# Attention's diagonal blocks multiplied with the 128 columns that count instead of 256

## The chip, the cores and the metric

The kernel runs on one core of a Trainium2 chip. The metric is the time of one execution in device microseconds (us). The time before is the median of three runs.

## What is computed

A decoder trunk of two layers over one sequence of 512 tokens with 2048 features, in float32. Layer 0 is differential attention: 8 heads, each with two components of queries and keys (128 wide) and one set of values (256 wide). Layer 1 is forgetting attention with 16 heads that are 128 wide; its keys, values and forget gates are projected once from the output of layer 0. Both attentions are causal. Cut to what matters here:

```
# layer 0, for block i of 128 queries, head h, component c
sc = q[i] @ k.T + alibi_bias             # (128 x 512), only keys s <= t count
p_c = softmax(where(causal, sc, -1e30))
o[i] = (p_0 - lam * p_1) @ v             # then rms_norm, silu gate, output projection
# layer 1, for block i of 128 queries, head h
sc = q[i] @ k.T + F[t] - F[s]
o[i] = softmax(where(causal, sc, -1e30)) @ v
```

Every layer ends with a residual sum and a LayerNorm; the inputs of the projections are scaled and shifted by vectors that come from a conditioning vector c.

## The kernel before

**Precision.** Each float32 matrix that is multiplied is split into a high and a low part of type float32r (F32R in the code). `products` (L171) then makes three matmuls that add into the same PSUM bank: high by high (L173), high by low (L174) and low by high (L175). Nearly all of the work of TensorE has one of these three lines. Transposes (L720, L767, L1163 and others) the sums of the modulation at the start (L503, L506) and one small product (L237) are the only matmuls that take tiles of plain F32.

**Projections.** `group` multiplies the 2048 x 512 input by 512 columns of weights at a time. It goes through sixteen k-tiles of 128 rows; each burst is two k-tiles for one of four PSUM banks, which is six matmuls of 512 moving columns. The weights come by `WeightStream`: a DMA on SP's queue, a cast on ScalarE (L93) and a subtraction on VectorE (L94).

**Attention, laid between the bursts.** After each burst `tick` runs one entry of the list `pieces`, and for the background products of the modulation one step of a generator. The pieces of a head are its scores, transposes and value products, in an order written out by hand (`attention_a` for layer 0, `attention_pair` for layer 1). So TensorE's order is fixed: six matmuls of a projection, then one piece, and so on.

**Scores.** `score(i)` multiplies query block i by the keys of blocks 0 to i, so w = (i + 1) * 128 columns count. The moving columns are n (layer 0, L692) or m (layer 1), which is w but at least 256. For i = 0 the matmul thus has 256 columns, and what follows on VectorE and ScalarE reads the first 128 of them.

**Values.** Layer 0 keeps the values as moving operand, 256 columns wide, in every block. Layer 1 has the transposed probabilities as moving operand (tiles pTh and pTl, filled by `turn`), and for key block j only queries from j * 128 on count. `values` starts its columns at t0 = min(j * 128, 256) (L1177), so the last block, j = 3, is multiplied with columns 256 to 511, of which the first 128 are blanks: L1090 and L1091 write zeros there once, before layer 1. A comment at L1089 says that this gives the rows 256 columns.

Of the kernel before, what the change touches and what calls it, by code (L numbers as in the profile page):

```python
# [13 lines left out]
ALU = mybir.AluOpType  # L14

P = 128
D = 2048
KT = D // P
T = 512
# [8 lines left out]
# Order of the start, see there: c sums of modulation, m their columns, t a k-tile of h, l its lower part,  # L28
# s a split of weights, g products of a k-tile, digits so many steps of the modulation's sums.
# [4 lines left out]
class Job:  # L34
    """A projection: runs of columns of a 2048-row weight matrix."""
# [14 lines left out]
class WeightStream:  # L50
    """Loads weights two k-tiles at a time and splits them into two float32r parts, ahead of their
    products."""
# [26 lines left out]
    def step(self, extra=None):  # L79
        """Splits the next two k-tiles; extra gives tiles for them outside the stream's own."""  # L80
        job, s = self.order[self.done]
        self.load(self.done + 1)
        st = self.stage[self.done]
        w = job.width
        if extra:
            hi, lo = ([extra() for _ in range(2)] for _ in range(2))
            for k in range(2):
                self.nc.scalar.copy(hi[k][:, :w], st[:, k, :w])
                self.nc.vector.tensor_tensor(lo[k][:, :w], st[:, k, :w], hi[k][:, :w].bitcast(F32), op=ALU.subtract)
        else:  # L90
            hi = self.pool.tile([P, 2, 512], F32R, name="whi", tag="whi", bufs=3)
            lo = self.pool.tile([P, 2, 512], F32R, name="wlo", tag="wlo", bufs=3)
            self.nc.scalar.copy(hi[:, :, :w], st[:, :, :w])  # L93
            self.nc.vector.tensor_tensor(lo[:, :, :w], st[:, :, :w], hi[:, :, :w].bitcast(F32), op=ALU.subtract)  # L94
            hi, lo = ([t[:, k, :] for k in range(2)] for t in (hi, lo))
        self.subs[(id(job), s)] = (hi, lo)
        self.done += 1
# [12 lines left out]
def tile_yoco(  # L110
# [60 lines left out]
    def products(dst, lhs, rhs, start, stop):  # L171
        """dst += lhs^T rhs with lhs and rhs as (hi, lo) parts."""
        PE.matmul(dst, lhs[0], rhs[0], start=start, stop=False)  # L173
        PE.matmul(dst, lhs[0], rhs[1], start=False, stop=False)  # L174
        PE.matmul(dst, lhs[1], rhs[0], start=False, stop=stop)  # L175

    # ---------------------------------------------------------------- constants
# [11 lines left out]
    # rows of parameters, turned into columns by the tensor engine  # L189
# [28 lines left out]
    rows = {}  # L218
# [22 lines left out]
    def rsqrt(y, v, n, pool):  # L241
        """y = v ** -0.5 by Newton steps from an estimate on the exponent."""
        t = pool.tile([P, n], I32, name="rs_t", tag=f"rs_t{n}", bufs=2)
        a = pool.tile([P, n], F32, name="rs_a", tag=f"rs_a{n}", bufs=2)
        h = pool.tile([P, n], F32, name="rs_h", tag=f"rs_h{n}", bufs=2)
        V.tensor_scalar(t, v.bitcast(I32), 1, None, op0=ALU.logical_shift_right)
        V.tensor_scalar(y.bitcast(I32), t, -1.0, float(0x5F3759DF), op0=ALU.mult, op1=ALU.add)
        V.tensor_scalar(h, v, -0.5, None, op0=ALU.mult)
        for _ in range(3):
            if n == 1:  # L250
                V.scalar_tensor_tensor(a, y, h, y, op0=ALU.mult, op1=ALU.mult)
            else:
                V.tensor_tensor(a, y, y, op=ALU.mult)
                V.tensor_tensor(a, a, h, op=ALU.mult)
            V.scalar_tensor_tensor(y, a, 1.5, y, op0=ALU.add, op1=ALU.mult)

    # ---------------------------------------------------------------- weight order
# [3 lines left out]
    # the first two heads: all but the keys of the second component, which follow for both at once  # L261
    first = {h: (Job(a_w_in, [(256 * h, 256), (2048 + 256 * h, 128)]), vg[h]) for h in range(2)}
    kk = Job(a_w_in, [(2048 + 128, 128), (2048 + 384, 128)])
    # k-tiles whose modulation is found together, and the order in which the two heads take k-tiles
# [6 lines left out]
    # the last columns for half of the tokens first, whose LayerNorm is then done ahead of the end  # L271
# [34 lines left out]
    def group(job, natural, evac, banks=range(4), bg=0, before_sub=None, after_sub=None, hold=0, after_held=None):  # L306
        """One projection; natural: tokens on the partitions, else features. The last hold weights
        stay until each bank has had them, one bank after the other."""
# [41 lines left out]
    # modulation vectors as columns [feature, k-tile]  # L350
# [4 lines left out]
    def mod_stream(segs, new_stage, new_acc, nk):  # L355
        """Vector-engine products of silu(c) with columns of a modulation matrix, 512 columns a
        segment; yields after each k-tile."""
# [38 lines left out]
    def mod_row(pool, ones_r, dst, bias, one):  # L396
        """Sums over the partitions, as ones^T acc with acc in two parts; in two steps."""
        def steps(acc):
            hi = pool.tile([P, 512], F32R, name="mhi", tag="mhi", bufs=1)
            lo = pool.tile([P, 512], F32R, name="mlo", tag="mlo", bufs=1)  # L400
            split(hi, lo, acc)
            row = pool.tile([1, 512], F32, name="mrow", tag="mrow", bufs=1)
            nc.sync.dma_start(row, bias.rearrange("(o n) -> o n", o=1))
            yield True
            pt = tr_bank()
            PE.matmul(pt, ones_r, hi, start=True, stop=False)
            PE.matmul(pt, ones_r, lo, start=False, stop=True)
            V.scalar_tensor_tensor(row, pt[0:1, :], one, row, op0=ALU.add, op1=ALU.add)
            nc.sync.dma_start(dst, row)
        return steps  # L410

    # ---------------------------------------------------------------- start: modulation and first projections
    # Shift and scale of sets of k-tiles: sums over silu(c) on the vector engine, for the first sets
    # half of them on the tensor engine. Each k-tile is multiplied for both heads; a head's partial
    # sums wait in SBUF while the other one's are in PSUM.
    part = {}
    with tc.tile_pool(name="start", bufs=2, reuse_waits="tile") as sp, tc.manual_schedule(engines={ET.DVE}):
# [12 lines left out]
        # one entry a tile: set, first k, number of k  # L430
# [53 lines left out]
        def dv(n):  # L484
            """n more products of modulation, none of them past the set after those summed."""
            while n and ahead[0] is not None and ahead[0] <= state["set"]:
                ahead[0] = next(steps, None)
                n -= 1
# [135 lines left out]
    # ---------------------------------------------------------------- layer 0: differential attention  # L624
# [53 lines left out]
    def attention_a(h, lead=3, late=()):  # L678
# [3 lines left out]
        def score(i, comp):  # L682
            def fn():
# [8 lines left out]
                n = max(w, 256)  # L692
# [3 lines left out]
                products(sc[:, :n], (q[0][:, ts], q[1][:, ts]), (k[0][:, :n], k[1][:, :n]), True, True)  # L696
# [110 lines left out]
    # head 1 waits until head 0 is done, and with it the values and gates of head 2  # L807
# [29 lines left out]
    # ---------------------------------------------------------------- output projections and LayerNorm  # L837
# [12 lines left out]
    def out_projection(jobs, layer, zp, opened, residual, norm, after_held=None):  # L850
        """z = residual + gate * y with the statistics of its rows; norm(b) follows a block's last
        columns. zp is filled by opened() once the pieces of the last head have been traced."""
# [43 lines left out]
    # h = x1 * scale + shift on n^T: x1 = n * g + b  # L896
# [19 lines left out]
    def build_half(s, half):  # L916
        """k-tiles 2s and 2s+1 of h for the keys and values, tokens of one half."""
# [17 lines left out]
        # the transposed tokens take the place of the others  # L935
# [3 lines left out]
    # the first values: the tokens of the second half are behind those of the first, which are ready earlier  # L939
# [25 lines left out]
    # ---------------------------------------------------------------- shared keys, values and forget gates  # L965
# [18 lines left out]
    # for each k-tile 64 columns: the two parts of the weights in columns 0-15 and 32-47. The products  # L984
    # take 128 columns, of which those 64 count.
# [26 lines left out]
    def forget_sums():  # L1012
        """-cumsum(min(z, 0) - log1p(exp(-|z|)))"""
# [6 lines left out]
        # log1p(e) = log(w) + (e - (w - 1)) / w  # L1020
# [63 lines left out]
    # ---------------------------------------------------------------- layer 1: forgetting attention  # L1084
# [4 lines left out]
    # the last block of keys is multiplied from query 256 on, so that its rows have 256 columns  # L1089
    V.tensor_scalar(pTh[:, 3, 256:384], mask[:, 0:P], 0.0, None, op0=ALU.mult)  # L1090
    V.tensor_scalar(pTl[:, 3, 256:384], mask[:, 0:P], 0.0, None, op0=ALU.mult)  # L1091
# [39 lines left out]
    def attention_b(hd):  # L1131
        st = {}

        def score(i):
            def fn():
                w = (i + 1) * P
                m = max(w, 256)
# [3 lines left out]
                products(sc[:, :m], (q[0][:, ts], q[1][:, ts]), (k[0][:, :m], k[1][:, :m]), True, True)  # L1141
# [28 lines left out]
        def values(j0, j1):  # L1170
            def fn():
# [4 lines left out]
                for j in range(j0, j1):  # L1176
                    t0 = min(j * P, 256)  # L1177
# [39 lines left out]
    # ---------------------------------------------------------------- layer 1: output projection and LayerNorm  # L1217
# [81 lines left out]
```

## Time and profile before

| | |
|---|---|
| median of three runs | 2016.39 us (2015.3 to 2018.02) |
| span of the profiled execution | 2017.1 us |
| TensorE, matmul instructions | 9115, busy 98% of the span |
| VectorE busy | 66% |
| ScalarE busy | 36% |
| DMA, mean over the span | 175 GB/s |

The times list no time of the profiled execution beside its span; the span is 0.7 us over the median of the three runs and inside their range. In the profile PE is TensorE's matmuls and PEld its weight loads, DVE is VectorE, ACT is ScalarE, SP the engine that issues most DMAs. A group of instructions is named by its tiles as out<-in; of a matmul the moving operand stands first, and 128*128 128x256 means 128 rows and columns of weights and 256 moving columns. The duration of a matmul in the profile overlaps that of the next, so the rate of a stream of matmuls is read from the distance between their starts in the timeline, not from the durations. The layers lie at these times: layer 0's attention from 228 to 860 us, keys and values from about 1030 to 1400 us, layer 1's attention from 1442 to 1857 us.

### The profile page before, as it was taken

The page shows a single profiled execution, that of the slowest core. Times are in us where ns is not written, and L with a number is a line of the kernel's source. Part 1 is how long each engine was busy: PE and PEld are TensorE (multiplying, and loading weights), DVE is VectorE, ACT ScalarE, POOL GpSimd, SP SyncE. Part 2 cuts the span into 40 slices and gives each one's busy share as a digit, 9 for nine tenths or more (in the row PEclk, how much of TensorE's full clock was granted, in tenths as well). Part 3 has the DMA queues.
Part 4 walks back from the last instruction along what each step waited for, and adds up shares of the span by engine and source line. Part 5 has one row for each costly group of instructions (what it writes and reads, how often), then busy time and mean ns, then how long its engine had stood idle before and what let it go on. Part 6 is the DMA issues. An engine that isn't in the chain of part 4 may idle for free.

```text
span 2017.1 us, 25055 instructions
## 1 busy us (share of the span) xinstructions
PE 1967.3 (98%) x9115; PEld 1627.0 (81%) x9115; DVE 1335.3 (66%) x2435; ACT 722.2 (36%) x1230; POOL 2.2 (0%) x10
## 2 busy tenths in 40 slices
PE   5999999999999999999999999999999999999997
PEld 4888878888878888888878877888888888888885
DVE  6887878777667677853575666645455555576678
ACT  2422444423333334431263222224333333453232
POOL 0000000000000000000000000000000000000000
PEclk8999999999999999999999999999999999999999
DMA  9994755564556565452344878733233323232754
GB/s 343 343 316 143 243 172 162 163 224 156 190 167 209 166 221 184 156 165 94 115 138 141 260 255 261 261 124 127 92 102 96 103 91 103 95 118 90 259 193 175
DMA packets 263095, 353.79 MB, mean 175 GB/s; under 512 B 18022, under 2 KB 162556, under 8 KB 262204
## 3 DMA queue, kind: packets, MB, share of 16 engines
q1 hardware_dynamic: 262896, 352.18, 53.3%
q8 instruction: 71, 1.16, 0.2%
q14 instruction: 52, 0.43, 0.1%
q10 hardware_dynamic: 76, 0.02, 0.0%
HBM read 339.47 MB, written 12.66 MB: 175 GB/s over the span
## 4 chain that ended last, share of the span: by engine, by line
PE 81%; DMA 8%; DVE 8%; issue 1%; SPq 1%; ACT 1%; DVEq 0%; ACTq 0%
PE acc L173 23%; PE acc L175 23%; PE acc L174 23%; DMA ms<-in_w_mod_dram 5%; DVE macc L386 2%; DVE wlo L94 2%; PE sc L174 2%; PE sc L175 2%; PE sc L173 2%; DMA sms<-in_w_mod_dram 1%; PE o L175 1%; PE o L174 1%; PE o L173 1%; PE tr L1163 1%; DMA ms<-in_kv_w_mod_dram 1%
## 5 line engine op out<-in xcount | busy, mean ns | idle before, releaser
L93 ACT CAST whi<-wst 128x1024 fp32r<-128x1024 f32 (+2 forms) x339 | 349.6, 1032 | 685.4 <-PE acc L175 315.6
L94 DVE TENSOR_TENSOR wlo<-wst,whi 128x1024 fp32r<-128x1024 f32 (+2 forms) x339 | 404.6, 1196 | 279.9 <-ACT whi L93 265.7
L173 PE MATMUL acc<-whi,hh 128*128 128x512 f32 x1252 | 494.6, 398 | 4.4 <-ACT vt L977 2.9
L174 PE MATMUL acc<-wlo,hh 128*128 128x512 f32 x1252 | 490.6, 392 | 0.1
L175 PE MATMUL acc<-whi,hl 128*128 128x512 f32 x1252 | 489.5, 391 | 0.0
L173 PE MATMUL acc<-hh,whi 128*128 128x512 f32 x1184 | 469.0, 396 | 3.6 <-ACT vt L977 2.9
L174 PE MATMUL acc<-hl,whi 128*128 128x512 f32 x1184 | 462.3, 390 | 0.0
L175 PE MATMUL acc<-hh,wlo 128*128 128x512 f32 x1184 | 462.3, 390 | 0.0
L386 DVE SCALAR_TENSOR_TENSOR macc<-ms,cact,macc 128x512 f32<-128x512 f32 x360 | 270.0, 750 | 116.2 <-DMA ms<-in_w_mod_dram 83.7
L173 PEld LDWEIGHTS acc<-whi,hh 128*128 128x128 f32 x1252 | 236.3, 189 | 51.5 <-ACT vt L977 4.2
L175 PEld LDWEIGHTS acc<-whi,hl 128*128 128x128 f32 x1252 | 235.8, 188 | 51.1 <-DVE hl L934 0.3
L174 PEld LDWEIGHTS acc<-wlo,hh 128*128 128x128 f32 x1252 | 236.2, 189 | 44.3 <-DVE wlo L94 0.5
L173 PEld LDWEIGHTS acc<-hh,whi 128*128 128x128 f32 x1184 | 222.6, 188 | 48.4 <-ACT vt L977 4.1
L175 PEld LDWEIGHTS acc<-hh,wlo 128*128 128x128 f32 x1184 | 222.5, 188 | 48.0
L174 PEld LDWEIGHTS acc<-hl,whi 128*128 128x128 f32 x1184 | 222.8, 188 | 41.1
L476 DVE SCALAR_TENSOR_TENSOR sacc<-sms,cact,sacc 128x512 f32<-128x512 f32 (+1 forms) x127 | 89.5, 705 | 5.9 <-DMA sms<-in_w_mod_dram 2.2
L1152 ACT ACTIVATE eb<-eb,mnb 128x128 f32<-128x128 f32 (+1 forms) x64 | 36.1, 564 | 96.7 <-DVE mnb L1149 95.6
L703 ACT ACTIVATE e<-e,mn 128x128 f32<-128x128 f32 (+3 forms) x64 | 36.1, 563 | 88.7 <-DVE mn L699 88.1
L1149 DVE CUSTOM_DVE_ANT_0 eb<-sc,biasb 128x128 f32<-128x128 f32 (+1 forms) x64 | 31.4, 490 | 52.8 <-PE sc L175 52.8
L1167 DVE TENSOR_TENSOR pTl<-tr,pTh 128x128 fp32r<-128x128 f32 (+1 forms) x64 | 31.2, 487 | 26.5 <-ACT pTh L1166 26.1
L1166 ACT CAST pTh<-tr 128x128 fp32r<-128x128 f32 (+1 forms) x64 | 27.1, 424 | 43.6 <-PE tr L1163 42.9
L769 ACT ACTIVATE ogT<-tr,subg 128x128 f32<-128x128 f32 x64 | 20.0, 364 | 56.0 <-PE tr L767 56.0
(251 smaller groups left out, 1740.0 us busy)
## 6 DMA issues: line engine op xcount, KB each, us to landing
wst<-in_a_w_in_dram SPq DMA_DIRECT2D x240, 256.0 KB
ms<-in_w_mod_dram SPq DMA_DIRECT2D x64, 512.0 KB
ms<-in_kv_w_mod_dram SPq DMA_DIRECT2D x64, 512.0 KB
wst<-in_kv_w_dram SPq DMA_DIRECT2D x64, 512.0 KB
ms<-in_w_mod_dram SPq DMA_DIRECT2D x128, 256.0 KB
wst<-in_b_w_in_dram SPq DMA_DIRECT2D x128, 256.0 KB
sms<-in_w_mod_dram SPq DMA_DIRECT2D x56, 512.0 KB
wst<-in_b_w_out_dram SPq DMA_DIRECT2D x48, 512.0 KB
```

Source lines behind the costliest of these rows:

```text
L93: self.nc.scalar.copy(hi[:, :, :w], st[:, :, :w])
L94: self.nc.vector.tensor_tensor(lo[:, :, :w], st[:, :, :w], hi[:, :, :w].bitcast(F32), op=ALU.subtract)
L173: PE.matmul(dst, lhs[0], rhs[0], start=start, stop=False)
L174: PE.matmul(dst, lhs[0], rhs[1], start=False, stop=False)
L175: PE.matmul(dst, lhs[1], rhs[0], start=False, stop=stop)
L386: V.scalar_tensor_tensor(acc, w, cact[:, kt : kt + 1], acc, op0=ALU.mult, op1=ALU.add)
L476: V.scalar_tensor_tensor(acc, w, sc, acc, op0=ALU.mult, op1=ALU.add)
L703: S.activation(e[:, :w], e[:, :w], AF.Exp, bias=mn, scale=-1.0, accum_out=rs)
L1149: V.tensor_tensor_reduce(out=e[:, :w], in0=sc[:, :w], in1=bias[:, :w], scale=-1.0, scalar=3.0e38, op0=ALU.add, op1=ALU.min, accum_out=mn)
L1152: S.activation(e[:, :w], e[:, :w], AF.Exp, bias=mn, scale=-1.0, accum_out=rs)
L1166: S.copy(pTh[:, 0 : i + 1, ts], src)
L1167: V.tensor_tensor(pTl[:, 0 : i + 1, ts], src, pTh[:, 0 : i + 1, ts].bitcast(F32), op=ALU.subtract)
```

## The change

Three places take the columns that count. `score` in both layers multiplies w columns, so block i = 0 has 128; `values` in layer 1 starts at j * 128, so block j = 3 has 128. The two instructions that wrote zeros into pTh and pTl are gone. The change also blanks comments and docstrings, which moves line numbers by a few.

```diff
@@ attention_a, score
                 w = (i + 1) * P
-                n = max(w, 256)
...
-                products(sc[:, :n], (q[0][:, ts], q[1][:, ts]), (k[0][:, :n], k[1][:, :n]), True, True)
+                products(sc[:, :w], (q[0][:, ts], q[1][:, ts]), (k[0][:, :w], k[1][:, :w]), True, True)
@@ layer 1: forgetting attention
-    # the last block of keys is multiplied from query 256 on, so that its rows have 256 columns
-    V.tensor_scalar(pTh[:, 3, 256:384], mask[:, 0:P], 0.0, None, op0=ALU.mult)
-    V.tensor_scalar(pTl[:, 3, 256:384], mask[:, 0:P], 0.0, None, op0=ALU.mult)
@@ attention_b, score
                 w = (i + 1) * P
-                m = max(w, 256)
...
-                products(sc[:, :m], (q[0][:, ts], q[1][:, ts]), (k[0][:, :m], k[1][:, :m]), True, True)
+                products(sc[:, :w], (q[0][:, ts], q[1][:, ts]), (k[0][:, :w], k[1][:, :w]), True, True)
@@ attention_b, values
-                    t0 = min(j * P, 256)
+                    t0 = j * P
                     products(st["o"][:, t0:], (vh[:, j, es], vl[:, j, es]), (pTh[:, j, t0:], pTl[:, j, t0:]), j == 0, j == 3)
```

## The prediction, made before the result was known

> **What bounds the kernel now.** I read the page of the profile first.
>
> ```profile
> span 2017.1 us, 25055 instructions
> PE 1967.3 (98%) x9115; PEld 1627.0 (81%) x9115; DVE 1335.3 (66%) x2435; ACT 722.2 (36%) x1230; POOL 2.2 (0%) x10
> ...
> PEclk8999999999999999999999999999999999999999
> ...
> PE 81%; DMA 8%; DVE 8%; issue 1%; SPq 1%; ACT 1%; DVEq 0%; ACTq 0%
> ```
>
> TensorE is busy 98% of the span at the full granted clock after the first slice, and its matmuls are 81% of the chain that ended last. That is an average, so I cut out the stretches that the change touches with the windows view: layer 0's attention, the stretch ahead of layer 1 (where the two fills of zeros are), and layer 1's attention. The columns are the window, its length, then busy time and number of instructions of each engine, the granted clock, the DMA share and rate.
>
> ```profile
> 228.00:860.00 632.00, 626.35 (x2968) 520.16 (x2967) 458.51 (x979) 247.18 (x504) 0.00 (x0) 1.00 0.57 182
> 1072.00:1442.00 370.00, 364.21 (x1599) 298.84 (x1598) 213.45 (x267) 104.75 (x128) 0.00 (x0) 1.00 0.61 197
> 1442.00:1857.00 415.00, 414.24 (x1998) 344.75 (x1997) 252.32 (x529) 170.08 (x317) 0.00 (x0) 1.00 0.31 99
> ```
>
> PE is idle 5.65 us of 632 in layer 0 and 0.76 us of 415 in layer 1, while VectorE works 459 and 252 us there. So in both stretches time added to or taken from the row of matmuls reaches the end nearly one for one. The small rest is absorbed where PE waits for something else. In layer 0 the waits view of PE puts most of it on one line, and the chain of waits shows short detours through DMA of the background products.
>
> ```profile
> PE tr L767 <- DVE og L753: 4.1, 4, 1.3
> ...
> 263.79 4.64 DMA ms<-in_w_mod_dram
> ...
> 564.66 4.06 DMA ms<-in_kv_w_mod_dram
> ```
>
> These are a few places; at them up to 5.65 us of added PE time could be hidden, or of saved PE time be lost.
>
> **How many matmuls change.** The groups by shape list those of 256 moving columns:
>
> ```profile
> L173 PE MATMUL sc<-k0h,q0h 128*128 128x256 f32 x16 | 4.4, 278 | 0.0
> L173 PE MATMUL sc<-k1h,q1h 128*128 128x256 f32 x16 | 4.4, 278 | 0.0
> ...
> L173 PE MATMUL sc<-kbh,qh 128*128 128x256 f32 x32 | 8.9, 279 | 0.0
> L173 PE MATMUL o<-pTh,vbh 128*128 128x256 f32 x32 | 8.9, 279 | 0.0
> ```
>
> In each group half go to 128 columns (block i = 0 of i = 0 and 1; block j = 3 of j = 2 and 3): 8 + 8 + 16 + 16 = 48 calls of `products`, each with three matmuls (L173 to L175). That is 48 matmuls in layer 0 and 96 in layer 1, 144 in all.
>
> **What a matmul costs in the row.** The durations of 278 ns overlap the next matmul, so I take distances between starts from the timeline. Columns: start, duration, engine, line, operation.
>
> ```profile
> 1516.73 0.34 PE L173 MATMUL sc<-kbh,qh 128*128 128x384 f32 x1
> 1516.91 0.34 PE L174 MATMUL sc<-kbl,qh 128*128 128x384 f32 x1
> 1517.08 0.34 PE L175 MATMUL sc<-kbh,ql 128*128 128x384 f32 x1
> 1517.26 0.40 PE L173 MATMUL acc<-hh,whi 128*128 128x512 f32 x1
> ...
> 1518.65 0.28 PE L173 MATMUL o<-pTh,vbh 128*128 128x256 f32 x1
> ...
> 1519.24 0.28 PE L175 MATMUL o<-pTh,vbl 128*128 128x256 f32 x1
> 1519.36 0.40 PE L173 MATMUL acc<-hh,whi 128*128 128x512 f32 x1
> ...
> 1521.87 0.39 PE L175 MATMUL acc<-hh,wlo 128*128 128x512 f32 x1
> ```
>
> Three matmuls of 384 columns take 1517.26 - 1516.73, 0.177 us each. The six of 256 columns (two key blocks, j = 2 and 3) take 1519.36 - 1518.65, 0.118 us each. From 1519.36 to 1521.87 there are eleven steps of 512 columns, 0.228 us each. So 128 columns are worth 0.051 us between 512 and 384 and 0.059 us between 384 and 256. The 144 matmuls cost 144 x 0.118 = 17.0 us now.
>
> No float32r matmul of fewer than 256 columns is in this trace, so the new price has to be bounded from its neighbours. The nearest ones are the plain F32 sums at the start, with a single moving column, and the transposes, with 128.
>
> ```profile
> 26.50 2.04 PE L503 MATMUL tr<-cact,sms 128*128 128x1 f32 x16
> ...
> L503 PEld LDWEIGHTS tr<-cact,sms x32: 187/192/303, 24.4 to 28.2; 128*128 128x128 f32 x32
> L503 PE MATMUL tr<-cact,sms x32: 165/250/353, 24.6 to 28.2; 128*128 128x1 f32 x32
> ...
> L506 PE MATMUL tr<-ones,sacc 128*128 128x1 f32 x64 | 8.6, 252 | 11.7 <-DVE sacc L476 11.7
> ...
> 1510.56 0.60 PE L1163 MATMUL tr<-ident,eb 128*128 128x128 f32 x4
> ```
>
> Two things are to be seen. First, a matmul with one column does not take its place in the row in no time: sixteen of them last 2.04 us, and less the last one's 0.35 us (its own end overlaps, its longest is 353 ns) that is 1.69 / 15 = 0.113 us from start to start. Four transposes last 0.60 us, and less one duration of 0.27 that is 0.33 / 3 = 0.11 us. Each has a weight load of its own, and one column streams in next to nothing, so 0.113 us is what a weight load of 128 columns takes of the row. Second, the code makes 16 calls at L503 and 32 at L506, but the trace has 32 and 64 records: a plain F32 product is served in two matmuls with a weight load each, while a float32r product is one (32 calls and 32 records in the group sc<-kbh,qh).
>
> So 256 columns, at 0.118 us, already stand on the floor of the weight load. The bounds of a product with 128 columns, from below: the straight line through the columns, 0.118 - 0.055 = 0.063 us; the weight load, 0.113 us; two matmuls as a plain F32 product has them, 2 x 0.113 = 0.226 us, or 2 x 0.118 = 0.236 us if each also streams like 256 columns; and at the top four loads, 4 x 0.113 = 0.452 us.
>
> **Which value I take.** One pass at full rate for four-byte operands has been seen in this trace only with 256 columns and more; the narrower true products it has, all plain F32, go the other way, in two matmuls. Nothing in the trace shows where a narrow float32r product belongs. I hold it likelier that the fast form needs the width and that a narrow product is done like plain F32, at about the price of a row of 512 columns, 0.228 us. This is a judgement, and the weakest step here. The sum: 144 x (0.228 - 0.118) = 15.8 us more. With 0.226 and 0.236 it is 15.6 and 17.0 us. If layer 0's 48 x 0.110 = 5.3 us all vanished in the 5.65 us of waits, 10.5 us would be left.
>
> The Trainium skill, FP8 and Floating Point Precision, section TensorE Precision Notes, says that true FP32 takes four passes through the array and that a reduced form reads four bytes and truncates; it names no width. Four passes over 128 columns would be a stream of 512, an estimate of 15.8 us more by the row of 512 columns; that L503 has two records a call agrees with more than one pass.
>
> **The other edits.** The two fills are 0.22 us each on VectorE at 1396 us:
>
> ```profile
> L1090 DVE TENSOR_SCALAR pTh<-mask 128x128 fp32r<-128x128 f32 x1 | 0.2, 221 | 0.0
> ```
>
> VectorE is idle 157 of 370 us in that window, and the trace names no instruction that waited for them: nothing. No wait is added: the scores need the same tiles, and the last value block reads only columns that `turn(3)` wrote, which it waited for before as well. Behind a score VectorE reads w columns as before; if the three matmuls take 0.33 us longer, the softmax starts that much later. Its result is wanted by a transpose two or more bursts later, and a burst is six steps of 0.228 us, 1.4 us, so this is hidden. If that cover were gone, it would cost 48 x 0.33 = 16 us again, which no row supports.
>
> **Rivals.**
>
> *The weight load is the floor (not slower).* The narrow product stays one matmul, and the next one waits for its weights: 144 x (0.113 - 0.118) = -0.7 us, 2015.7 us. It decides as soon as the fast form holds at 128 columns. For it speaks that one column and 128 columns both come at 0.11 us; against it only that no float32r row shows it.
>
> *The columns count all the way (faster).* Weight loads are pulled far enough ahead, and the price follows the line: 144 x (0.063 - 0.118) = -7.9 us, 2008.5 us. Against it: the rows of L503, whose loads had nothing to wait for and still came at 0.113 us. The Trainium skill, TensorE: Matmul & The Clock Gate, section Back-to-back issue gap, gives about 81 ns for each matmul of 128 columns in a stream of loads and matmuls; by it the estimate is 144 x (0.081 - 0.118) = -5.3 us. The rows of L503 do not agree with that page so far, though they are plain F32.
>
> *Four loads (much slower).* Each pass brings its own weights: 144 x (0.452 - 0.118) = 48 us, 2064 us. Against it: plain F32 shows two records a call, not four.
>
> **How the numbers follow.** I add to the median of the runs, 2016.4 us; the span of the profiled execution, 2017.1 us, lies 0.7 us above it, inside the runs' 2015.3 to 2018.0. The forecast is 2016.4 + 15.8 = 2032.2 us, with a chance of 0.66; its own range is 2025.8 (10.5 us on the lowest run) to 2035.0 (17.0 us on the highest). The weight floor gets 0.20, the line 0.08, four loads 0.06. A measurement of this kernel can tell about 0.2%, 4 us, from no change. The range has to take in the floor (0.7 us under the lowest run is 2014.6) and ends at 2035.0; the line and the four loads, 0.14 together, are left out. Slower is 0.66 + 0.06 = 0.72, within 0.2% is 0.20, faster is 0.08.
>
> **What would show it.** In the changed profile the groups with 128x128 on L173 to L175 decide. By the forecast their starts in the timeline lie 0.23 us apart, with a duration near the 390 ns of 512 columns or with two records for each call, and PE's busy time grows in the two attention windows, by about 5 us in layer 0 and 10.6 us in layer 1. By the weight floor they lie 0.11 us apart with one record each and the windows stay. By the line they lie 0.06 us apart. I am wrong if the starts stay at or below 0.12 us, or if the rows get slower and the span does not follow, because the 5.65 us of waits in layer 0 and more elsewhere took it up.

## The result, and the profile after

The changed kernel takes 2025.0 us (median of 7 runs, 2023.02 to 2029.31), the kernel before 2018.57 us (median of 7). The ratio is 1.0033, with a 95% interval of 1.0024 to 1.0043: 6.7 us slower. The profiled execution took 2026.14 us with a span of 2024.4 us.

The page of the changed kernel, its span, its busy times and the chain:

```profile
span 2024.4 us, 25068 instructions
...
PE 1969.8 (97%) x9115; PEld 1625.4 (80%) x9115; DVE 1333.6 (66%) x2433; ACT 721.9 (36%) x1230; POOL 2.2 (0%) x10
...
PE 73%; DVE 12%; DMA 10%; issue 2%; ACT 1%; SPq 1%; DVEq 0%; ACTq 0%
```

The number of matmuls is the same. TensorE's part of the chain fell from 81% to 73%, and VectorE and DMA took it over. The matmuls' busy time grew by 2.5 us (from 1967.3) and the span by 7.3 us, so most of the loss is waiting. The windows view of the changed kernel shows where:

```profile
228.00:860.00 632.00, 619.02 (x2921) 510.69 (x2920) 449.89 (x953) 242.05 (x496) 0.00 (x0) 1.00 0.57 181
1442.00:1857.00 415.00, 414.56 (x1999) 345.04 (x1998) 254.33 (x529) 172.16 (x319) 0.00 (x0) 1.00 0.32 99
```

PE's idle time in layer 0 went from 5.65 to 13.0 us, and in the same 632 us it makes 47 fewer matmuls. In layer 1 nothing got worse: 0.44 us idle, 0.76 before.

**The price of a narrow product.** The timeline of the changed kernel around a score of block 0, with the weight loads (PEld):

```profile
1504.19 0.39 PE L175 MATMUL acc<-hh,wlo 128*128 128x512 f32 x1
1504.19 0.19 PEld L173 LDWEIGHTS sc<-kbh,qh 128*128 128x128 f32 x1
1504.42 0.22 PE L173 MATMUL sc<-kbh,qh 128*128 128x128 f32 x1
1504.42 0.19 PEld L174 LDWEIGHTS sc<-kbl,qh 128*128 128x128 f32 x1
1504.47 0.28 PE L174 MATMUL sc<-kbl,qh 128*128 128x128 f32 x1
1504.53 0.19 PEld L175 LDWEIGHTS sc<-kbh,ql 128*128 128x128 f32 x1
1504.59 0.27 PE L175 MATMUL sc<-kbh,ql 128*128 128x128 f32 x1
1504.64 0.19 PEld L173 LDWEIGHTS acc<-hh,whi 128*128 128x128 f32 x1
1504.70 0.44 PE L173 MATMUL acc<-hh,whi 128*128 128x512 f32 x1
...
1504.98 0.40 PE L174 MATMUL acc<-hl,whi 128*128 128x512 f32 x1
```

A score of block 0 of the kernel before, which had 256 columns (the first head of layer 1; the lines above are of a later head):

```profile
1442.52 0.28 PE L173 MATMUL sc<-kbh,qh 128*128 128x256 f32 x1
...
1442.88 0.40 PE L173 MATMUL acc<-hh,whi 128*128 128x512 f32 x1
...
1443.11 0.40 PE L174 MATMUL acc<-hl,whi 128*128 128x512 f32 x1
```

Each narrow product is one record. The weight loads start every 0.11 us (1504.42, 1504.53, 1504.64, 1504.75 for the next), and the matmuls follow them: the three take 0.28 us in place of 0.36. Part of that is given back, because the weights for the successor of the wide product behind them begin to load only at 1504.75, 0.05 us after that product, which takes 0.28 us in place of 0.23. To the second matmul of the projection it is 0.56 us after and 0.59 us before: 0.03 us saved for three products, 0.01 us each (the medians over all scores of this kind in the two traces are 0.564 and 0.586 us). That is the weight floor of the rivals, not the price of the forecast.

**Where the time went.** The first and last starts of the first product of a score, in the answer on the tile sc (last columns: first to last start). First the kernel before, then the changed one:

```profile
L173 PE MATMUL sc<-kbh,qh x64: 277/308/398, 1442.5 to 1850.6; 128*128 128x256 f32 x32, 128*128 128x384 f32 x16, 128*128 128x512 f32 x16
...
L173 PE MATMUL sc<-k0h,q0h x32: 276/306/390, 228.8 to 850.2; 128*128 128x256 f32 x16, 128*128 128x384 f32 x8, 128*128 128x512 f32 x8
```

```profile
L173 PE MATMUL sc<-kbh,qh x64: 220/307/393, 1450.6 to 1857.5; 128*128 128x128 f32 x16, 128*128 128x256 f32 x16, 128*128 128x384 f32 x16, 128*128 128x512 f32 x16
...
L173 PE MATMUL sc<-k0h,q0h x32: 220/333/389, 229.0 to 860.0; 128*128 128x128 f32 x8, 128*128 128x256 f32 x8, 128*128 128x384 f32 x8, 128*128 128x512 f32 x8
```

Layer 0's scores begin 0.2 us later and end 9.8 us later. Between them and layer 1 1.7 us come back (8.1 us late at 1450.6), and layer 1's scores take 406.9 us in place of 408.1. So layer 0 loses 9.6 us, though its products got cheaper. 7.3 us of it are idle time of PE. The rest lies in stretches that count as busy; one product of 256 columns there that comes behind a wait, at 233.08 us, has its successor 0.23 us later in place of 0.118. Each trace is one execution, so differences of a microsecond or two between them mean little.

**What waits in layer 0.** The waits of PE in the changed kernel from 228 to 860 us:

```profile
PE tr L766 <- DVE og L752: 3.7, 4, 1.5
PE tr L719 <- DVE ss L749: 3.7, 4, 1.8
PE o L175 <- DVE al L169: 1.8, 3, 0.8
PE tr L719 <- DVE e L710: 1.2, 2, 0.8
```

These are the first four of the list, and all are waits for VectorE's share of the attention. VectorE itself waits most for ScalarE's casts of the weights (L94, 59.2 us before and 57.2 after), which did not grow, and then for DMAs; its waits for these from 228 to 870 us, of the kernel before and then of the changed one:

```profile
DVE macc L386 <- DMA ms<-in_kv_w_mod_dram: 26.3, 28, 3.2
DVE macc L386 <- DMA ms<-in_w_mod_dram: 17.8, 20, 2.4
DVE macc L384 <- DMA ms<-in_w_mod_dram: 1.8, 1, 1.8
```

```profile
DVE macc L386 <- DMA ms<-in_kv_w_mod_dram: 31.1, 30, 3.4
DVE macc L386 <- DMA ms<-in_w_mod_dram: 27.3, 23, 2.4
```

macc are the background sums of the modulation, ms the tile of weights that a DMA brings for two of them. The waits grew from 45.9 to 58.4 us. What stands behind a waiting sum in VectorE's list waits too, as the timelines below show. And the list is another one. Both programs as built have, among 2305 instructions on VectorE, 177 at another place, 27 of 1040 on SP, 11 of 9066 on TensorE and 8 of 1074 on ScalarE; nearly all lie in layer 0. The kernel's text does not write out this order; the build makes it, and the narrower products gave another. VectorE's list at the first head, in the build before (left) and after (right), in the first query block's softmax:

```
L94  wlo                        L94  wlo
L699 e,mn  128x128              L386 macc   <- ahead of the softmax
L699 mn                         L698 e,mn  128x128
L386 macc                       L698 mn
L707 rsum  (reciprocal)         L386 macc
L708 rsum                       L706 rsum  (reciprocal)
L710 e     128x128              L386 macc   <- ahead of the softmax
L386 macc                       L707 rsum
L711 e     128x128              L709 e     128x128
```

The same places in the timelines of VectorE, with the last step of ScalarE (ACT) that the second reciprocal needs; the bracket is the idle time before the instruction and what ended it. Before:

```profile
230.45 0.75 DVE L386 SCALAR_TENSOR_TENSOR macc<-ms,cact,macc 128x512 f32<-128x512 f32 x1 [1.59 <-DMA ms<-in_w_mod_dram]
231.12 0.28 DVE L699 CUSTOM_DVE_ANT_0 e<-sc,bias 128x128 f32<-128x128 f32 x1
...
232.47 0.28 DVE L699 CUSTOM_DVE_ANT_0 e<-sc,bias 128x128 f32<-128x128 f32 x1
...
233.34 0.16 DVE L707 RECIPROCAL rsum<-rsum 128x2 f32<-128x2 f32 x1
...
236.69 0.19 ACT L703 ACTIVATION_READ_ACCUMULATOR e<-e,mn 128x1 f32 x1
...
236.91 0.17 DVE L707 RECIPROCAL rsum<-rsum 128x2 f32<-128x2 f32 x1 [0.67 <-ACT e L703]
```

After:

```profile
232.07 0.75 DVE L386 SCALAR_TENSOR_TENSOR macc<-ms,cact,macc 128x512 f32<-128x512 f32 x1 [2.40 <-DMA ms<-in_w_mod_dram]
232.74 0.28 DVE L698 CUSTOM_DVE_ANT_0 e<-sc,bias 128x128 f32<-128x128 f32 x1
...
234.75 0.28 DVE L698 CUSTOM_DVE_ANT_0 e<-sc,bias 128x128 f32<-128x128 f32 x1
...
235.38 0.75 DVE L386 SCALAR_TENSOR_TENSOR macc<-ms,cact,macc 128x512 f32<-128x512 f32 x1 [0.34 <-DMA ms<-in_w_mod_dram]
236.05 0.16 DVE L706 RECIPROCAL rsum<-rsum 128x2 f32<-128x2 f32 x1
...
238.59 0.19 ACT L702 ACTIVATION_READ_ACCUMULATOR e<-e,mn 128x1 f32 x1
...
240.45 0.75 DVE L386 SCALAR_TENSOR_TENSOR macc<-ms,cact,macc 128x512 f32<-128x512 f32 x1 [2.31 <-DMA ms<-in_w_mod_dram]
241.12 0.16 DVE L706 RECIPROCAL rsum<-rsum 128x2 f32<-128x2 f32 x1
```

The second reciprocal comes at 236.91 us before and at 241.12 us after: 4.2 us later, though the head's first score starts only 0.14 us later. It stands right behind a sum that waited 2.31 us for its DMA, where before it waited only for ScalarE. What it needs from ScalarE was there at 238.78 us (238.59 + 0.19), so it stood ready for 2.3 us behind that sum.

Not all of the 4.2 us is the order. 1.6 us are there at the first softmax instruction (component 0, 231.12 and 232.74 us), which stands ahead of the list above, and up to it VectorE's list is the same in both builds. In the traces of the runs below, that instruction starts 2.2 to 2.5 us behind the first score with the new order and 2.1 to 3.0 us with the old one; the 3.8 us of this execution stand alone. From there to the second reciprocal the order tells: 5.7 to 5.8 us in the four traces in which VectorE has the old order there, 7.8 to 8.6 us in the five in which it has the new one.

### The profile page after: what moved, and what is told of

Its sections match the earlier page's. It is cut to its first block, busy times and chain, and to the rows that moved or that the text cites. A ratio compares the mean times of both kernels' runs of the same rounds, so it can differ in the third digit from the quotient of the medians.

```text
span 2024.4 us, 25068 instructions
## 1 busy us (share of the span) xinstructions
PE 1969.8 (97%) x9115; PEld 1625.4 (80%) x9115; DVE 1333.6 (66%) x2433; ACT 721.9 (36%) x1230; POOL 2.2 (0%) x10
## 4 chain that ended last, share of the span: by engine, by line
PE 73%; DVE 12%; DMA 10%; issue 2%; ACT 1%; SPq 1%; DVEq 0%; ACTq 0%
PE acc L173 21%; PE acc L174 21%; PE acc L175 21%; DMA ms<-in_w_mod_dram 7%; DVE macc L386 3%; DVE wlo L94 3%; DMA ms<-in_kv_w_mod_dram 2%; PE sc L174 1%; PE sc L173 1%; PE sc L175 1%; PE o L175 1%; PE o L174 1%; PE o L173 1%; PE tr L1158 1%; ACT whi L93 1%
## 5 line engine op out<-in xcount | busy, mean ns | idle before, releaser
L94 DVE TENSOR_TENSOR wlo<-wst,whi 128x1024 fp32r<-128x1024 f32 (+2 forms) x339 | 404.6, 1196 | 278.3 <-ACT whi L93 273.4
```

## The experiments

My theory after this: the price of the products is the weight floor, and the loss is the order of layer 0, through VectorE's wait for the background's DMAs. Its rival: the products themselves cost time, by their price or by when their results come.

To tell order from products I fixed the order: each instruction is tied behind the one that should precede it on its engine, issue order alone. The edit, in short, for any kernel and any order:

```diff
+for engine, places in ORDER:                      # places among the instructions traced for it
+    for last, this in zip(places, places[1:]):
+        tc.add_manual_dep(own[engine][this], own[engine][last].name, NoSync)
```

**Half of the change: layer 0's scores.** `n = max(w, 256)` becomes `n = w`, nothing else.

> Only layer 0's scores take w columns; layer 1 is as before. In this build the order in which VectorE, ScalarE, TensorE and SP's queue get their instructions during layer 0 is that of the changed kernel, which differs from before. Order theory: the loss lies in that order, so nearly all of it is here: 7 to 10 us slower than before. Price theory (a narrow product costs 0.23 us, and something else gave time back): 48 x 0.11 = 5.3 us at most. Weight floor alone, with no effect of the order: 0.4 us faster.

Measured: 1.0034 (1.0023 to 1.0045), 6.9 us slower, just under the 7 to 10 us that I expected: within the noise all of the loss.

**The other half: layer 1.** Scores, values and fills of layer 1 as in the change, layer 0 as before.

> Only layer 1 is changed (scores, values, no fills of zeros); layer 0 is as before and its instructions stand in the same order as before. Order theory with the weight floor: 32 groups of three at 0.024 us saved each, 0.8 us faster, which is within 0.2% of before. Price theory: 96 x 0.11 = 10.6 us slower. Line theory: 96 x 0.055 = 5.3 us faster.

Measured: 1.0004 (0.9995 to 1.0012), the same as before within 0.2%. The 10.6 us of the forecast's price and the 5.3 us of the line are both outside the interval, -1.0 to 2.4 us.

**The changed products in the old order.** The changed kernel with ORDER taken from the build before.

> The changed kernel, but each engine and SP's queue issue their instructions in the order that the kernel before has; 128 columns in all 144 products. Order theory with the weight floor: 48 groups of three at 0.024 us saved, 1.2 us faster than before, and the waits of PE in layer 0 are back at about 6 us. If the narrow products themselves cause the loss, by price or by when their results come, it stays 6 to 7 us slower.

Measured: 1.0001 (0.9992 to 1.0009), the loss is gone with the same 144 narrow products. PE is idle 7.3 us of the 632 in layer 0, near the 6 that I expected and far from 13.0. The expected gain of 1.2 us is inside the interval and not shown.

**The old products in the new order.** The kernel before with ORDER taken from the changed build.

> The kernel before with its 256 columns and its two fills of zeros, but each engine and SP's queue issue their instructions in the order that the changed kernel has. Order theory: 7 to 9 us slower than before, as slow as the changed kernel or 1 us slower still. If the narrow products cause the loss: the same as before.

Measured: 1.0025 (1.0015 to 1.0036), 5.0 us slower, with not one product changed. It is 2 us less than I expected, but the interval overlaps with that of the changed kernel. These two crossed runs settle that the order makes the loss.

**The new order in the first head alone.** The changed kernel; ORDER is new up to VectorE's place 415 and old from there.

> The changed kernel with 128 columns; the new order holds for the first head of layer 0 (instruction places up to VectorE's 415th), the old order from there on. In the two runs with the whole new order the first head has 3.6 and 5.0 us of the loss. Order theory: 2.5 to 4 us slower than before (3.6 to 5 less 1.2 us for the cheaper products). If the loss comes of the whole order and not of a place: under 1.5 us slower.

Measured: 1.0020 (1.0010 to 1.0030), 4.0 us slower, as expected. A good part of the loss comes from the first head; since the interval runs from 2.0 to 6.1 us, it is not shown that it is more than half. VectorE's waits for the DMAs of the background come to 47.9 us here, 2.0 more than before, while PE is idle 9.6 us in place of 5.65.

**The new order on VectorE alone.** TensorE, ScalarE and SP keep the old one.

> The changed kernel with 128 columns; VectorE has the new order, and TensorE, ScalarE and SP's queue have the old one. If the loss starts in VectorE (sums of the background products that stand ahead of the softmax and wait there for their DMA): nearly all of it, 4 to 7 us slower than before. If it starts in SP's queue (loads of the background's weights that stand ahead of the loads of the projection's weights): within 1.5 us of before.

Measured: 1.0124 (1.0109 to 1.0139), 25 us slower: the way that I expected and four times the size. The waits of VectorE for the DMAs of the background in this run (228 to 876 us) show where:

```profile
DVE macc L386 <- DMA ms<-in_w_mod_dram: 34.4, 26, 6.6
DVE macc L386 <- DMA ms<-in_kv_w_mod_dram: 31.0, 29, 2.3
```

With 4.2 us of L384 they come to 69.6 us, 23.7 more than before. The longest wait for in_w_mod_dram is 6.6 us, against 2.4 us in both builds. My reading, which no run takes apart, is that VectorE asks for sums early whose loads SP, in the old order, issues late, so that the two lists belong together. The run does not say how the loss of the changed kernel divides between the lists. The new order on SP alone was not tried.

**The wait for the DMAs taken away.** The sums of layer 0 read a tile that is already there; the DMAs run as before. It leaves out the modulation that the sums should give. One run in the old order, one in the new.

```diff
-                w = t[:, kk, :] if nk > 1 else t
+                w = dist if nk > 1 else t
```

> The changed kernel in the old order; the background sums of layer 0 on VectorE read one tile that is already there instead of the tile that a DMA loads, and the DMAs still run. So the modulation that these sums give is another one. Both theories: the wait of VectorE for these DMAs (44 us in layer 0 before) is gone, PE's waits in layer 0 fall by up to 5 us, 2 to 6 us faster than before.

> The same as the run old_order_no_dma_wait (background sums of layer 0 on a tile that is already there, another modulation), but in the new order. If the new order loses time through VectorE's wait for these DMAs: the difference between the two orders falls from 6 us to under 2 us. If the new order loses by something else (VectorE's work itself standing in a worse order, SP's queue): the difference stays at 4 to 7 us.

Measured: old order 0.9976 (0.9966 to 0.9987), 4.8 us faster than before; new order 0.9971 (0.9960 to 0.9981), 5.9 us faster. The new order is no longer slower. The windows view from 228 to 860 us, old order and then new order:

```profile
228.00:860.00 632.00, 631.14 (x3005) 525.31 (x3004) 458.30 (x978) 251.42 (x511) 0.00 (x0) 1.00 0.57 183
```

```profile
228.00:860.00 632.00, 631.16 (x3005) 525.18 (x3004) 457.88 (x978) 251.44 (x514) 0.00 (x0) 1.00 0.57 184
```

PE is idle 0.9 and 0.8 us. With the wait gone, the same list that cost 7.3 us more of idle PE costs nothing. From the first softmax instruction to the second reciprocal it is 6.3 us in both. The edit also frees the buffers sooner, so SP's queue does not wait for VectorE either; these two were not separated.

**A try at a faster kernel.** The same memory as four buffers of one k-tile, three loads ahead, with 128 and with 256 columns.

```diff
-        lambda: ap.tile([P, 2, 512], F32, name="ms", tag="ms", bufs=2),
+        lambda: ap.tile([P, 512], F32, name="ms", tag="ms", bufs=4),
...
-        2,
+        1, 3,    # one k-tile a load, three loads ahead
```

> The changed kernel (128 columns); the background weights of layer 0 come in four buffers of one k-tile, three loads ahead, in the same memory instead of two buffers of two k-tiles, one ahead. A buffer is free after one sum instead of two, so the loads are asked for earlier. The order is the one that comes out of this build. If VectorE's wait for these loads is what costs: that wait falls below 30 us in layer 0 and the kernel is 3 to 7 us faster than before, since without the wait it was 5 us faster. If smaller loads take as long to land, or SP's doubled issues delay the projection's weights: 0 to 10 us slower than before.

> The kernel before (256 columns) with the same four buffers of one k-tile for the background weights of layer 0. Expected: 2 to 6 us faster than before, and within 2 us of the run fine_loads_128, because without the wait for the loads the order no longer matters and 128 columns are worth 1.2 us. If the order still matters, the two are more than 4 us apart.

Measured: 1.0038 (1.0024 to 1.0051) with 128 columns and 1.0011 (1.0002 to 1.0020) with 256: 7.7 and 2.2 us slower, so the gain that I expected fell in both. With 128 columns the other case that I had written down came, 0 to 10 us slower; its reason is not shown. VectorE's wait for the loads did fall, to 30.2 us from 58.4 and to 29.3 from 45.9, and yet nothing was won: PE is idle 9.7 and 6.0 us in layer 0. So the sum of these waits does not measure the loss; that it matters which instruction stands behind them is my reading. The two lie 5.5 us apart, and their traces again show two different lists on VectorE. The order is the likely cause, but these two were not crossed. No version here that computes the result beats the kernel before.

**The price by itself.** The kernel before, with two blocks of layer 1's values cut into pieces of 128 columns.

```diff
-                    products(st["o"][:, t0:], ..., (pTh[:, j, t0:], pTl[:, j, t0:]), j == 0, j == 3)
+                    step = P if j in (1, 2) else T - t0
+                    for u in range(t0, T, step):
+                        us = slice(u, u + step)
+                        products(st["o"][:, us], ..., (pTh[:, j, us], pTl[:, j, us]), j == 0, j == 3)
```

> The kernel before, but in layer 1's values the blocks j = 1 (384 columns) and j = 2 (256 columns) are multiplied in pieces of 128 columns: 240 narrow products in place of 48 of 384 and 48 of 256 columns, which cost 48 x 0.177 + 48 x 0.118 = 14.2 us. The order of layer 0 is as before. Weight floor (0.112 us each): 26.9 - 14.2 = 12.7 us slower. Line (0.063 us): 1 us slower. Price of the forecast (0.228 us): 40 us slower.

Measured: 1.0060 (1.0045 to 1.0074), 12.1 us slower (9.1 to 14.9), where the weight floor gave 12.7, the line 1 and the forecast's price 40. By groups:

```profile
L175 PE MATMUL o<-pTh,vbl 128*128 128x128 f32 x80 | 22.0, 275 | 0.0
L174 PE MATMUL o<-pTl,vbh 128*128 128x128 f32 x80 | 22.0, 275 | 0.0
L173 PE MATMUL o<-pTh,vbh 128*128 128x128 f32 x80 | 20.3, 253 | 0.0
```

There are 80 records for 80 calls: one matmul for each narrow product. Where narrow products follow each other, their starts lie 0.111 us apart in the median.

## Why the prediction was right or wrong

The direction was right by luck: its reason was wrong, and 15.8 us were forecast where 6.7 came.

**What bounds the kernel:** right as far as it was tried. In layer 1 the added time of the split values reached the end nearly one for one (12.1 us of 12.7), and in layer 0 the 7.3 us of added waits did. That saved time of matmuls reaches the end as well is not shown; 1.2 us was too little to see.

**The number of products, 144:** right.

**"Which value I take":** this step failed first. I held that a narrow float32r product is done like plain F32, at 0.228 us. It is one matmul and takes 0.11 us, the distance at which the weight loads start. The bounds had held this value, and the rows of plain F32 that I quoted gave it as 0.113 and 0.11 us; I set a judgement that no row carried above a row that was there. The term of the sum should have been that of the rival, -0.7 us; the runs with the order held fixed and the layer-1 half show nothing else than that within their intervals.

**"The other edits ... No wait is added":** this step failed second, and it is the one that made the loss. The data that each instruction needs were looked at, and they are unchanged; the order of the lists was taken as fixed. The description of the kernel says that TensorE's order is fixed by the pieces, and of TensorE that nearly holds (11 of 9066). VectorE's list, where the sums and the softmax are mixed, was not written out by hand, and it moved. Of the rivals none had this mechanism. That no wait was added in the text and all the same 12.5 us more of VectorE's waiting for loads came, and 7.3 us more of PE's, is the lesson of this case. The term that stood at nothing is the whole 6.7 us.

**The line and the four loads:** both fell, on the split values and on layer 1. The Trainium skill, TensorE: Matmul & The Clock Gate, section Back-to-back issue gap, gives about 81 ns for a matmul of 128 columns in a stream; these rows have 0.11 us, so for float32r products the page does not hold here. At that price the split values would have come out 240 x 0.081 - 14.2 = 5.2 us slower, an estimate outside their interval of 9.1 to 14.9 us. Its section LDWEIGHTS (loading the stationary operand), the number of columns divided by 1.2, gives 107 ns for 128 columns, and the starts of the loads, 0.11 us apart, agree, while the records give each load a duration of 0.19 us.

**The range** held the time by luck as well, since it took in the weight floor for its low end. The mechanism that filled it was not one of its cases.

What stays open: whether it is the weight load that sets the 0.11 us, since every matmul in these traces has a load of its own; what in the build turns a narrower product into another order, and how the loss divides between VectorE's list and SP's.

## What to carry to other kernels

Where the build orders the instructions, a change of shape in one place can change the lists of other engines in other places; compare the lists before the times are explained, and run the change in the old order and the old code in the new order. Look where background work that waits for a DMA stands in its engine's list: here a reciprocal whose input was ready at 238.78 us started at 241.12, behind such a sum. Moving only these sums behind the softmax was not tried. And where every product loads new weights, 128 columns in place of 256 save 0.01 us here.

## What the runs showed of the hardware

A float32r product of 128 columns, with new weights, takes its place in the row in 0.11 us and 256 columns in 0.118 us, so with new weights for every product 128 columns win almost nothing over 256. In the records the first of three narrow products behind a wide one takes only 0.05 us to the next start (1504.42 to 1504.47; the median over such scores is 0.058), which speaks for the load and against a minimum of the matmul itself as what sets the 0.11 us, and the wide product behind the last one pays that back with 0.28 us in place of 0.23.
